# Nine seven-product steps in place of six, half of the other low parts by an accumulating DMA, and a new layout of the buffers

## The chip, the cores and the metric

The kernel runs on one core of one Trainium2 chip. The metric is the time of one execution on the device in microseconds (us). Three runs of the kernel before gave 1803.22, 1807.13 and 1808.31 us; the median is 1807.13 us.

## The reference

With DEPTH = 1 the reference computes one attention layer between two normalisations, in float32, for 256 positions and 4096 channels:

```python
h = x                                             # 256 x 4096
xn = rms_norm(h, norm_attn)
q, k, v, g = split(xn @ w_in, 4)                  # w_in 4096 x 16384
z = q_head @ k_head.T / sqrt(128)                 # 32 heads of 128
log_fail = where(causal, log_sigmoid(-z), 0)
a = where(causal, exp(log_sigmoid(z) + suffix_sums(log_fail)), 0)
h = h + ((a @ v_head) * silu(g)) @ w_out          # w_out 4096 x 4096
out = rms_norm(h, final_norm)
```

## The kernel before, in words

**Three matmuls for one product.** TensorE (PE) works on float32r operands, so each float32 operand is split into a high part (a cast) and a low part (what the cast lost). A product is `mm3`, L422 to L428: high times high, high of the input times low of the weights (`wl`), low of the input times high of the weights (`wh`), all 128x512 columns here. The high part of the weights is made by ScalarE (ACT) at L172, the low part by VectorE (DVE) through `minus`, L98.

**Units, steps, parts.** The work is a list of 21 units. Units 0 to 15 are the input projection, two for each group j of four heads: unit 2j gives q and k of the group, unit 2j+1 gate and v. Units 16 to 18 are the output projection, two blocks of 512 columns each; units 19 and 20 are one block each. I number the units from 0, so an odd unit below 16 is a gate-and-v unit. A unit has 16 steps s over the 4096 input channels; a step takes 256 channels and a quad of weights, 128 partitions x 4 x 512, loaded as `raw` (two DMAs of 512 KB on SP's queue, L150, three buffers).

A unit multiplies a 2 by 2 arrangement of blocks. Units 0 and 16 do it plainly, units 19 and 20 are single blocks, and the other 14 input units (2 to 15) and units 17 and 18 are mixed: in most steps eight products ("eight" steps, `EIGHT_PARTS`: two parts of 1024 columns), in the steps listed in `SEVEN` seven products of sums and differences of blocks ("seven" steps, `SEVEN_PARTS`: parts of 1024, 512, 1024 and 1024 columns). A seven step needs three additions of weight blocks by DVE, in place in `raw` (L160, L163, L164), ahead of its third part. Banks 1, 6 and 7 of PSUM hold sums that only seven steps add to; `combine_early` and `combine_late` (L346 to L363) put the banks together at a unit's end.

**What sets the order.** The loop at L687 walks through the parts. Before it issues the products of part n it calls `split` for as many later parts as the buffers allow: up to PAIRS = 4 parts of 1024 columns and SINGLES = 1 of 512, counted from part n. Work of the attention heads is hung on steps in a table `todo` (L569 to L664): transposes (`heads_T`), scores, sums (`weights_of`) and `heads_out` for each of the four heads of a group, the gate and the split of v. Each engine then runs its own instructions in a fixed order; the names `wl322`, `wh322` are the low and high part of part 322, `raw125` the quad 125. The heads' results go to DRAM (`spill`, L497), come back in units 15 and 16 as plain forms and as the seven forms (`build`, L213), and once more in unit 18.

## Time and profile before

| what | us |
|---|---|
| median of 3 runs | 1807.13 |
| the profiled execution | 1806.54 |
| its span, first to last instruction | 1804.6 |
| PE busy | 1778.2 |
| DVE busy | 1495.3 |
| ACT busy | 1089.5 |
| span of two mixed input units in the steady part | 177.1 |

The span lies 1.9 us under the execution's time; what happens in the trace is told from the span's start. Busy times of an engine count overlapping instructions once. Means of single instructions overlap their successors: the profile gives a matmul of 512 columns 390 ns, while matmuls start every 0.23 us.

### The profile page before, as it was taken

The numbers are of one execution on the slowest core, as the hardware profiler recorded it, in microseconds if no ns is written. First come the engines' busy times: TensorE is split into PE (matmuls) and PEld (weight loads), VectorE is DVE, ScalarE is ACT, GpSimd is POOL, SyncE is SP. The second block draws the span as 40 slices with busy tenths as digits, with TensorE's granted clock in tenths as the row PEclk, the third lists the DMA queues.
The fourth block names the chain that finished last, engine by engine and source line by source line (L and its number), as shares of the span: only waits on it lengthen the run. The fifth ranks groups of instructions, "written<-read, shape, count | busy, mean of one in ns | idle before, by whom it ended". The sixth has DMA issues, their size and how long they took to land. (4 is left out here: it accounts for less than half of the span.)

```text
span 1804.6 us, 22433 instructions
## 1 busy us (share of the span) xinstructions
PE 1778.2 (99%) x8107; PEld 1469.9 (81%) x8107; DVE 1495.3 (83%) x1810; ACT 1089.5 (60%) x1449; POOL 39.5 (2%) x80
## 2 busy tenths in 40 slices
PE   8999999999999999999999999999999999999997
PEld 6888788888888888888888888888887888788885
DVE  5678988888888888888888888888888977889854
ACT  5765665666566656665666565656565756655642
POOL 0000000000000000000000000000001011000000
PEclk9999999999999999999999999999999999999999
DMA  8856555555555545555555555555556666656664
GB/s 313 304 197 223 197 182 195 190 193 197 188 205 191 195 177 216 192 194 184 196 202 186 196 196 193 187 192 190 195 194 221 241 231 219 236 220 239 245 228 150
DMA packets 108814, 374.25 MB, mean 207 GB/s; under 512 B 12704, under 2 KB 12960, under 8 KB 108704
## 3 DMA queue, kind: packets, MB, share of 16 engines
q1 hardware_dynamic: 102960, 354.46, 54.8%
q0 software_dynamic: 5600, 18.35, 3.1%
q8 instruction: 63, 1.03, 0.2%
q14 instruction: 47, 0.39, 0.1%
q10 hardware_dynamic: 144, 0.02, 0.0%
HBM read 364.40 MB, written 8.39 MB: 207 GB/s over the span
## 5 line engine op out<-in xcount | busy, mean ns | idle before, releaser
L172 ACT CAST wh<-raw 128x1024 fp32r<-128x1024 f32 (+1 forms) x833 | 818.8, 1001 | 609.7 <-PE acc L428 274.8
L98 DVE TENSOR_TENSOR wl<-raw,wh 128x1024 fp32r<-128x1024 f32 (+1 forms) x833 | 950.6, 1159 | 245.0 <-ACT wh L172 236.5
L426 PE MATMUL acc<-wh,nh 128*128 128x512 f32 x1708 | 672.9, 394 | 2.2 <-ACT v_sb L383 1.9
L427 PE MATMUL acc<-wl,nh 128*128 128x512 f32 x1708 | 666.4, 390 | 2.7 <-DVE wl L98 2.3
L428 PE MATMUL acc<-wh,nl 128*128 128x512 f32 x1708 | 666.3, 390 | 0.0
L427 PEld LDWEIGHTS acc<-wl,nh 128*128 128x128 f32 x1708 | 321.1, 188 | 68.7 <-DVE wl L98 5.6
L428 PEld LDWEIGHTS acc<-wh,nl 128*128 128x128 f32 x1708 | 320.6, 188 | 68.0
L426 PEld LDWEIGHTS acc<-wh,nh 128*128 128x128 f32 x1708 | 320.9, 188 | 66.4 <-ACT v_sb L383 2.3
L426 PE MATMUL acc<-wh,ph 128*128 128x512 f32 x324 | 125.8, 390 | 2.1 <-ACT wh L172 1.5
L427 PE MATMUL acc<-wl,ph 128*128 128x512 f32 x324 | 126.5, 391 | 0.1
L428 PE MATMUL acc<-wh,pl 128*128 128x512 f32 x324 | 126.1, 389 | 0.0
L160 DVE TENSOR_TENSOR raw<-raw 128x1024 f32<-128x1024 f32 x96 | 117.4, 1223 | 2.3
L426 PE MATMUL acc<-wh,sh 128*128 128x512 f32 x256 | 101.3, 396 | 4.4 <-DVE sh L205 4.4
L427 PE MATMUL acc<-wl,sh 128*128 128x512 f32 x256 | 100.9, 394 | 0.7 <-DVE wl L98 0.6
L428 PE MATMUL acc<-wh,sl 128*128 128x512 f32 x256 | 100.4, 393 | 0.0
L426 PEld LDWEIGHTS acc<-wh,ph 128*128 128x128 f32 x324 | 60.7, 188 | 16.2 <-ACT wh L172 2.7
L427 PEld LDWEIGHTS acc<-wl,ph 128*128 128x128 f32 x324 | 60.8, 188 | 14.0 <-DVE wl L98 1.4
L428 PEld LDWEIGHTS acc<-wh,pl 128*128 128x128 f32 x324 | 60.8, 188 | 12.6
L164 DVE TENSOR_TENSOR raw<-raw 128x512 f32<-128x512 f32 x96 | 66.2, 690 | 2.4
L163 DVE TENSOR_TENSOR raw<-raw 128x512 f32<-128x512 f32 x96 | 66.1, 688 | 1.7
L426 PEld LDWEIGHTS acc<-wh,sh 128*128 128x128 f32 x256 | 48.7, 190 | 15.0 <-ACT wh L172 5.1
L427 PEld LDWEIGHTS acc<-wl,sh 128*128 128x128 f32 x256 | 48.8, 191 | 11.5 <-DVE wl L98 1.5
(167 smaller groups left out, 1374.1 us busy)
## 6 DMA issues: line engine op xcount, KB each, us to landing
raw<-in_w_in_dram SPq DMA_DIRECT2D x510, 512.0 KB, 4.2
raw<-in_w_out_dram SPq DMA_DIRECT2D x128, 512.0 KB, 4.2
xn<-in_xT_dram POOLq DMA_DIRECT2D x16, 256.0 KB, 3.0
xr<-in_x_dram SPq DMA_DIRECT2D x16, 256.0 KB, 5.0
spill<-gated POOLq DMA_DIRECT2D x16, 256.0 KB, 4.1
o<-spill POOLq DMA_DIRECT2D x16, 256.0 KB, 3.6
p<-spill POOLq DMA_DIRECT2D x16, 256.0 KB, 3.8
xres<-in_x_dram SPq DMA_DIRECT2D x16, 256.0 KB, 4.3
```

The lines of the kernel that those rows point to most:

```text
L98: nc.vector.tensor_tensor(out=out_, in0=full, in1=part.bitcast(F32), op=ALU.subtract)
L160: nc.vector.tensor_tensor(out=r[:, 0:3:2, :], in0=r[:, 0:4:3, :], in1=r[:, 2:3, :].broadcast_to([P, 2, CW]), op=ALU.add)
L163: nc.vector.tensor_tensor(out=r[:, 3, :], in0=r[:, 0, :], in1=r[:, 3, :], op=ALU.add)
L164: nc.vector.tensor_tensor(out=r[:, 1, :], in0=r[:, 3, :], in1=r[:, 1, :], op=ALU.add)
L172: nc.scalar.copy(wh[n][:, c, :], f)
L426: nc.tensor.matmul(out_, ah, bh, start=start, stop=False, **kw)
L427: nc.tensor.matmul(out_, ah, bl, start=False, stop=False, **kw)
L428: nc.tensor.matmul(out_, al, bh, start=False, stop=stop, **kw)
```

## The change

It does the following.

- `SEVEN` grows from six steps to nine (2, 3, 5, 6, 8, 9, 11, 12, 13) in units 2 to 15 and to eight in units 17 and 18 (`SEVEN_OUT`, without 12).
- In an eight step the low part of the second part of 1024 columns is no longer made by DVE. One quad ahead, ACT writes the negated high part into the buffer (`sum_up`, L165 of the changed kernel), and a DMA from GpSimd (POOL) adds the weights from DRAM to it with `accum_op` (L167). There are 114 such DMAs of 512 KB.
- The buffers of 1024 columns: four of high parts as before; three of low parts (`LOWS`) in place of four, and two more (`SUMMED`) that only the second part of a step other than a seven uses. The loop's condition counts them apart.
- Other tiles share buffers or get fewer: one buffer in place of two for `f`, four in place of five for `v`, the forms built in place of their source, the gate's transposes made head by head in `heads_out`, the scratch of the squares in PSUM.
- The heads' steps move: transposes at steps 5 and 10 of an odd unit in place of 2 and 8, and later steps in the next unit. Each pair of heads is now split once into high and low part (`heads_parts`) and stored in DRAM three times, so that the plain forms come back by DMA (`load_parts`) without a split; the forms of units 17 and 18 are built up to step 1 of unit 17.
- At the start x goes first: its first block on ACT's queue and ahead of all else, then weights and x by turns on SP's queue. The plain units copy bank 3 ahead of bank 7.

The diff, cut to what these points and the prediction speak of:

```diff
-SEVEN = (2, 4, 6, 9, 11, 13)
+SEVEN = (2, 3, 5, 6, 8, 9, 11, 12, 13)
+SEVEN_OUT = (2, 3, 5, 6, 8, 9, 11, 13)
 RAW_BUFS = 3
 PAIRS = 4
+LOWS = 3
+SUMMED = 2
 SINGLES = 1
...
+    summed = {p["quad"]: n for n, p in enumerate(parts) if p["summed"]}
+
+    def sum_up(q):
+
+        if q not in summed:
+            return
+        n = summed[q]
+        wl[n] = wp.tile([P, KT, CW], F32R, tag="wd", name=f"wl{n}", bufs=SUMMED)
+        nc.scalar.activation(wl[n], raw[q][:, parts[n]["place"], :], AF.Copy, scale=-1.0)
+        w, c, s = quads[q][1]
+        nc.gpsimd.dma_start(wl[n], w[c, s], accum_op=ALU.add)
+
     def split(n):
         p = parts[n]
         q = p["quad"]
         if p["i"] == 0 and (n == 0 or parts[n - 1]["quad"] != q):
             load(q + RAW_BUFS - 1)
+            sum_up(q + 1)
...
-        tag, bufs = ("w", PAIRS) if size == KT else ("one", SINGLES)
-        wh[n] = wp.tile([P, size, CW], F32R, tag=tag + "h", name=f"wh{n}", bufs=bufs)
-        wl[n] = wp.tile([P, size, CW], F32R, tag=tag + "l", name=f"wl{n}", bufs=bufs)
+        place, size = p["place"], p["size"]
+        (hi, hb), (lo, lb) = (("wh", PAIRS), ("wl", LOWS)) if size == KT else (("oneh", SINGLES), ("onel", SINGLES))
+        wh[n] = wp.tile([P, size, CW], F32R, tag=hi, name=f"wh{n}", bufs=hb)
+        if p["summed"]:
+            nc.scalar.copy(wh[n], r[:, place, :])
+            return
+        if p["apart"]:
+            lo, lb = "wd", SUMMED
+        wl[n] = wp.tile([P, size, CW], F32R, tag=lo, name=f"wl{n}", bufs=lb)
...
+        for k in range(KT):
+            nc.scalar.dma_start(xs[i][:, k, :], xT[i][:, k, :])
+            if k == 0:
+                nc.scalar.dma_start(gcol, gain_in)
...
-        for dst, r, col in ((one, r1, 1), (two, r2, 2)):
-            for t in range(NT):
...
+        for dst, r, col, t in ((one, r1, 1, 0), (one, r1, 1, 1), (two, r2, 2, 1), (two, r2, 2, 0)):
+            nc.scalar.activation(dst[t], bank[PLAIN[f"C{t + 1}{col}"]], AF.Copy, scale=r[:, t : t + 1])
...
-        for i, s in ((0, 2), (1, 8)):
+        for i, s in ((0, 5), (1, 10)):
             at(u + 1, s, heads_T, j, i)
             at(u + 1, s + 1, scores, j, i)
             at(u + 1, s + 3, weights_of, j, i)
...
-            inside = [len(range(*parts[m]["place"].indices(2 * KT))) for m in range(n, ready + 1)]
-            if inside.count(KT) > PAIRS or inside.count(1) > SINGLES:
+            inside = parts[n : ready + 1]
+            pairs = [m for m in inside if m["size"] == KT]
+            apart = sum(m["apart"] for m in pairs)
+            if len(pairs) > PAIRS or apart > SUMMED or len(pairs) - apart > LOWS or len(inside) - len(pairs) > SINGLES:
                 break
```

How this moves instructions is shown at one place on three engines: the end of step 12 and step 13 of unit 7, a gate-and-v unit in the steady part.

First DVE. Before, step 12 is an eight step (`wl318`, `wl319`) and step 13 a seven step on `raw125`; `a3_1` and `al3_1` belong to the group's second head:

```order
L98 TENSOR_TENSOR wl318_6026<-raw124_5927,wh318_6025 128x1024
L98 TENSOR_TENSOR wl319_6036<-raw124_5927,wh319_6035 128x1024
L98 TENSOR_TENSOR wl321_6056<-raw125_5953,wh321_6055 128x512
L98 TENSOR_TENSOR wl320_6052<-raw125_5953,wh320_6051 128x1024
L160 TENSOR_TENSOR raw125_5953<-raw125_5953 128x2x512
L466 TENSOR_TENSOR a3_1_6069<-a3_1_6069,bound_110 128x256
L163 TENSOR_TENSOR raw125_5953<-raw125_5953 128x512
L164 TENSOR_TENSOR raw125_5953<-raw125_5953 128x512
L98 TENSOR_TENSOR al3_1_6074<-a3_1_6069,ah3_1_6073 128x384
L98 TENSOR_TENSOR wl322_6081<-raw125_5953,wh322_6080 128x1024
L98 TENSOR_TENSOR wl323_6097<-raw125_5953,wh323_6096 128x1024
```

Of the change, where step 12 is a seven step too (ahead of these rows stand its first two low parts `wl352` and `wl353` with `qkl3_1` of the head between them, and its three additions):

```order
L101 TENSOR_TENSOR wl354_6252<-raw124_6143,wh354_6251 128x1024
L101 TENSOR_TENSOR wl355_6279<-raw124_6143,wh355_6278 128x1024
L448 SCALAR_TENSOR_TENSOR f3_1_6268<-z3_1_6261,f3_1_6268 128x384
L101 TENSOR_TENSOR wl356_6295<-raw125_6161,wh356_6294 128x1024
L450 TENSOR_TENSOR f3_1_6268<-f3_1_6268,bound_110 128x256
L101 TENSOR_TENSOR wl357_6302<-raw125_6161,wh357_6301 128x512
L178 TENSOR_TENSOR raw125_6161<-raw125_6161 128x2x512
L101 TENSOR_TENSOR fl3_1_6275<-f3_1_6268,fh3_1_6274 128x384
L181 TENSOR_TENSOR raw125_6161<-raw125_6161 128x512
L101 TENSOR_TENSOR wl358_6315<-raw125_6161,wh358_6314 128x1024
L182 TENSOR_TENSOR raw125_6161<-raw125_6161 128x512
L101 TENSOR_TENSOR wl359_6325<-raw125_6161,wh359_6324 128x1024
```

The additions of step 12 came in, the second half of the head's scores now stands between the parts of step 13, and the last addition L182 stands right before the last low part.

Next ACT, at the last high parts of step 13 (`wh322`, `wh323` before; `wh358`, `wh359` in the change). Before:

```order
L172 CAST wh322_6080<-raw125_5953 128x1024
L469 CAST ah3_1_6073<-a3_1_6069 128x384
L172 CAST wh323_6096<-raw125_5953 128x1024
L172 CAST wh324_6115<-raw126_6022 128x1024
L349 COPY v_sb3_0_6187<-acc7_1_5615 128x512
```

And in the change, where `wl363` is the negated high part of step 15:

```order
L194 CAST wh358_6314<-raw125_6161 128x1024
L364 COPY v_sb3_0_6420<-acc7_1_5806 128x512
L165 ACTIVATE wl363_6337<-raw127_6288 128x1024
L466 ACTIVATE a3_1_6375<-z3_1_6261 128x384
L365 ACTIVATE g_sb3_6419<-acc7_1_5806 128x512
L194 CAST wh359_6324<-raw125_6161 128x1024
```

Two copies of bank 1, a negation and a head's activation moved in front of the cast of the step's last part.

Last PE, at the end of step 13. `nh13` and `nl13` are the input's high and low part of step 13, `nh14` that of step 14. Before:

```order
L426 MATMUL acc7_4_5531<-wh323_6096,nh13_1679 128x512
L427 MATMUL acc7_4_5531<-wl323_6097,nh13_1679 128x512
L428 MATMUL acc7_4_5531<-wh323_6096,nl13_1680 128x512
L426 MATMUL acc7_6_5650<-wh323_6096,nh13_1679 128x512
L427 MATMUL acc7_6_5650<-wl323_6097,nh13_1679 128x512
```

In the change:

```order
L429 MATMUL acc7_4_5718<-wh359_6324,nh13_1672 128x512
L429 MATMUL acc7_6_5847<-wh359_6324,nh13_1672 128x512
L429 MATMUL acc7_2_5711<-wh360_6340,nh14_1738 128x512
L430 MATMUL acc7_4_5718<-wl359_6325,nh13_1672 128x512
L431 MATMUL acc7_4_5718<-wh359_6324,nl13_1673 128x512
L430 MATMUL acc7_6_5847<-wl359_6325,nh13_1672 128x512
```

Two matmuls that need only high parts, one of them of step 14, moved ahead of the first that needs the low part `wl359`.

More of the change, by code (lines that the diff above doesn't have):

```diff
@@ L131 @@
                     dict(u=u, s=s, i=i, last=i == len(which) - 1, place=place, prods=prods, quad=len(quads) - 1,
-                         seven=which is SEVEN_PARTS)
+                         seven=which is SEVEN_PARTS, summed=which is EIGHT_PARTS and i == 1,
+                         size=len(range(*place.indices(2 * KT))),
+                         apart=which is not SEVEN_PARTS and (s % 2 if kind == "single" else i) == 1)
                 )
@@ L262, in build_xn @@
             )
[L263 to L267 removed]
+        build(i, y, SEVEN, "n")
+    load_x(0)
+    load(0)
+    load_x(1)
+    load(1)
     load_x(2)
```

209 lines of the change are left out of this document (94 added, 115 removed).

## The prediction

> **What bounds the kernel now.** I read the page's first two lines first, then the table of waits for the whole core, then busy time by stretches.
>
> ```profile
> span 1804.6 us, 22433 instructions
> PE 1778.2 (99%) x8107; PEld 1469.9 (81%) x8107; DVE 1495.3 (83%) x1810; ACT 1089.5 (60%) x1449; POOL 39.5 (2%) x80
> ...
> ACT wh L172 <- PE acc L428: 274.8, 308, 2.5
> DVE wl L98 <- ACT wh L172: 236.5, 305, 3.0
> ...
> PE acc L426 <- DVE sh L205: 4.4, 1, 4.4
> ...
> PE acc L427 <- DVE wl L98: 2.9, 3, 1.4
> ...
> PE acc L426 <- ACT v_sb L383: 1.9, 1, 1.9
> ```
>
> PE is busy for 1778.2 of 1804.6 us. The long waits are those of the other engines: ACT waits 308 times until PE has freed a buffer of high parts, and DVE then waits for ACT. So both work as far ahead as their buffers let them, and PE sets the time. PE's own waits are a handful, 4.4 us of them at the start. Next, two stretches: two input units in the steady part, and one output unit.
>
> ```profile
> 446.50:623.60 177.10, 177.10 (x822) 147.58 (x821) 152.86 (x173) 109.43 (x140) 1.08 (x2) 1.00 0.54 194
> ...
> 1612.00:1695.00 83.00, 83.00 (x367) 68.44 (x366) 75.03 (x83) 49.03 (x62) 3.22 (x6) 1.00 0.67 237
> ```
>
> After the length come the busy times of PE, PEld, DVE, ACT and POOL, the granted clock and the DMA share. In 177.1 us PE never stops, and DVE is busy for 152.9. **PE's matmul count is the time here, and DVE has 24 us of room in two units.**
>
> **Term 1, matmuls taken away.** Three more sevens in each of 14 mixed input units and two more in each of two mixed output units: (14 x 3 + 2 x 2) x 3 = 138 matmuls of 512 columns fewer; the order of PE shows the same 138.
>
> ```profile
> 445.47 0.39 PE L427 MATMUL acc<-wl,nh 128*128 128x512 f32 x1
> ...
> 448.89 0.39 PE L427 MATMUL acc<-wl,nh 128*128 128x512 f32 x1
> ```
>
> These two starts lie 15 matmuls and 3.42 us apart, 0.228 us each (a mean of 390 ns overlaps the next one). 138 x 0.228 = **31.5 us less**, as long as PE stays fed. A seven step is 21 matmuls, 4.79 us; an eight step 24, 5.47 us.
>
> **Term 2, what DVE must now do, and when.** Durations overlap on DVE too, so I take the distance from start to start.
>
> ```profile
> 695.19 1.23 DVE L160 TENSOR_TENSOR raw<-raw 128x1024 f32<-128x1024 f32 x1
> 696.45 0.69 DVE L163 TENSOR_TENSOR raw<-raw 128x512 f32<-128x512 f32 x1
> ...
> 706.10 1.23 DVE L160 TENSOR_TENSOR raw<-raw 128x1024 f32<-128x1024 f32 x1
> 707.24 0.42 DVE L466 TENSOR_TENSOR a<-a,bound 128x256 f32<-128x256 f32 x1
> 707.58 0.69 DVE L163 TENSOR_TENSOR raw<-raw 128x512 f32<-128x512 f32 x1
> 708.30 0.69 DVE L164 TENSOR_TENSOR raw<-raw 128x512 f32<-128x512 f32 x1
> 708.91 0.55 DVE L98 TENSOR_TENSOR al<-a,ah 128x384 fp32r<-128x384 f32 x1
> 709.38 2.35 DVE L98 TENSOR_TENSOR wl<-raw,wh 128x1024 fp32r<-128x1024 f32 x2
> ...
> 715.70 1.22 DVE L98 TENSOR_TENSOR wl<-raw,wh 128x1024 fp32r<-128x1024 f32 x1 [0.79 <-ACT wh L172]
> 716.84 0.68 DVE L351 TENSOR_TENSOR v_sb<-acc,v_sb 128x512 f32<-128x512 f32 x1
> 717.44 1.22 DVE L98 TENSOR_TENSOR wl<-raw,wh 128x1024 fp32r<-128x1024 f32 x1
> ```
>
> A low part of 1024 columns takes 1.14 us (715.70 to 716.84), one of 512 takes 0.60, of 384 0.47, of 256 0.34. The three additions, each needing the one before, take 1.26 + 0.72 + 0.61 = 2.59 us; with other work between them 1.14 + 0.60 + 0.60. A seven step therefore costs DVE 3 x 1.14 + 0.60 + 2.59 = 6.6 us against PE's 4.79; an eight step costs it 2.28 before and 1.14 after the change (ACT and a DMA make the other low part), against 5.47. Over two input units DVE gains 2 x (3 x 2.59 + 3 x 0.60 - 4 x 1.14) = 10.0 us and two splits of heads (1.2): 152.9 + 11.2 = 164 of the 172.9 us that PE would need (177.1 - 18 x 0.228). As a sum it fits. **As an order it does not.** Sevens drain DVE's lead, and a lead is bounded by the buffers: three low parts and one single, that is one seven step. The eights 14, 15, 0, 1 leave DVE idle once those are full, and steps 2 to 13 hold nine sevens.
>
> I walk through the worst place, steps 11, 12, 13 of an odd unit, with the fullest lead: when PE starts step 11, DVE has all of 11. Its rows from there to the last low part of 13 (front part, first order block) are six of 1024 (6.84), two of 512 (1.20), additions 2.59 and 2.34, and the heads' 0.60 + 0.47 + 0.34 + 0.47 = 1.88: 14.85 us. It starts 1.30 us late, since the buffer of 12's first low part is that of 11's (four matmuls and 0.39), and before the last low part it waits for a cast that follows L182. The rows of ACT:
>
> ```profile
> 705.63 0.49 ACT L463 ACTIVATE a<-z 128x384 f32<-128x384 f32 x1 [0.82 <-PE z L460]
> ...
> 709.08 1.05 ACT L172 CAST wh<-raw 128x1024 fp32r<-128x1024 f32 x1 [0.26 <-DVE raw L164]
> ...
> 712.12 0.58 ACT L349 COPY v_sb<-acc 128x512 f32<-128x512 f32 x1
> ...
> 713.55 0.59 ACT L350 ACTIVATE g_sb<-acc 128x512 f32<-128x512 f32 x1
> ```
>
> So DVE ends at 1.30 + 14.85 + 1.05 = 17.2 us. PE wants that part after two steps (9.58), 15 matmuls (3.42), one more (0.23) and the heads' matmuls. For those:
>
> ```profile
> 404.99 0.28 PE L426 MATMUL o<-ah,vh 128*128 128x256 f32 x1
> ...
> 405.63 0.44 PE L426 MATMUL acc<-wh,nh 128*128 128x512 f32 x1
> ```
>
> Six such cost 0.64; a head's scores have the same shapes, its four sums about 0.6 (an estimate from this row). 9.58 + 3.42 + 0.23 + 0.64 + 0.6 = 14.5: DVE is 2.7 us late. In the changed order PE takes products with high parts ahead of their turn just there (third block), worth about three matmuls, 0.7: 2.0 us remain. The same sum in an even unit is 14.73 + 1.3 = 16.0 against 14.4, late by 1.6, and 0.9 after the products taken ahead. Mean of the two: 1.45.
>
> Two things come on top. ACT runs its queue in order, and the changed order has a cast of v, a negation, an activation of the head and a cast of g between the last two casts of high parts (second block): 1.05 + 0.58 + 1.05 + 0.49 + 0.59 = 3.76 us (the negation taken as a cast of its size) after L178, against 2.8 of DVE's work: 0.95 us in odd units, 0.5 in the mean. Behind that wait stand wh359, then wl359, then PE. And in the pairs 2-3, 5-6, 8-9 the same sum leaves 8.44 - (1.30 + 6.6) = 0.5 us, while up to 1.3 us of head work stands in them: from nothing to 0.9 late each, 1.2 per unit taken. So a unit is late by 1.45 + 0.5 + 1.2 = 3.15 us, **14 x 3.15 = 44 us more**. Bounds: 0.7 if the products taken ahead hide all but the triple, 5.9 if each wait of ACT for additions also stops DVE. The point of no gain is (31.5 + 5) / 14 = 2.6, the 5 from the next term. Output units have no such shortage: eight sevens there, and DVE has 8 of 83 us free.
>
> **Term 3, start and seams.**
>
> ```profile
> 8.97 0.35 DVE L205 TENSOR_SCALAR sh<-xs,gcol 128x256 fp32r<-128x256 f32 x1 [3.28 <-DMA xs<-in_xT_dram]
> ...
> 9.47 0.76 PE L426 MATMUL acc<-wh,sh 128*128 128x512 f32 x1 [4.35 <-DVE sh L205]
> ```
>
> The first product waits for x, queued on SP behind four weight loads; from ACT's queue it leaves about 2 us earlier: 3 us less with the loads that no longer stand before it, and 0 to 5 as bounds. The plain units free bank 3 one copy sooner (0.6 of the 1.9 us row above), and the forms of the output units come by DMA or are built later: 1.4. Together **5 us less**.
>
> **Term 4, the low part by DMA**, costed at nothing. It is covered by PE's work from the free buffer to its use: in a run of eights one step, half a step and a matmul, 5.47 + 2.74 + 0.23 = 8.4 us. To be hidden: a negation (1.05), the issue on POOL (0.54, the last row below) and the landing.
>
> ```profile
> raw<-in_w_in_dram SPq DMA_DIRECT2D x510, 512.0 KB, 4.2
> ...
> spill<-gated POOLq DMA_DIRECT2D x16, 256.0 KB, 4.1
> o<-spill POOLq DMA_DIRECT2D x16, 256.0 KB, 3.6
> ...
> L502 POOL DMA_DIRECT2D o<-spill x16: 536/536/543, 1297.2 to 1527.0; - x16
> ```
>
> No row shows an accumulating DMA. From below it is the plain load of its size, 4.2; from above that twice, for it reads its target too, 8.4. I take 5.5, nearer to the plain row: 7.1 of 8.4 us. At the upper end the part is 1.6 us late, in steps 0 and 1 of each unit. Behind such an accumulation on POOL's queue stand the next one and the spills; behind the negation on ACT stand the casts of the next step. The Trainium skill, page "DMA: Bandwidth & Descriptors", section "Anatomy of one DMA — SWDGE (gpsimd) path", gives 2.0 us plus the bytes at 436 GB/s for a DMA issued from GpSimd, 3.2 us by estimate at 512 KB; by that price the term stays nothing and rival 2 has no chance. It would make 2.6 of the 256 KB that take 3.6 and 4.1 in this trace, so the measured rows decide and rival 2 stays.
>
> **Sum**, against the profiled execution: 1804.6 - 31.5 + 44 - 5 = 1812 of span, and 1.9 around it (1806.5 - 1804.6): **1814 us**. The execution lies 0.6 under the median of 1807.1.
>
> **Rivals.**
> 1. Faster: the lead is enough. For it: DVE's sum fits with 9 us to spare, and PE's reordering may hide more than I count. Against: 2 us of the triple don't go away by it. With lateness between 0 and 2.2 us per unit: 1770 to 1801, about 1790.
> 2. Slower by far: the low part lands late. With 8.4 us landing, 2 x 1.6 x 14 = 45 us on top: 1859. It decides from a landing of 6.8 us on (8.4 - 1.6). For it: the DMA share is 0.54 already, and two units load 33.6 MB and get 7.3 MB more (14 low parts), read twice at worst.
> 3. Waits that halve the clock.
>
> ```profile
> 13.02 0.63 PE L426 MATMUL acc<-wh,sh 128*128 128x512 f32 x1
> 13.44 0.63 PE L427 MATMUL acc<-wl,sh 128*128 128x512 f32 x1
> ...
> 15.11 0.39 PE L427 MATMUL acc<-wl,sh 128*128 128x512 f32 x1
> 15.34 0.40 PE L428 MATMUL acc<-wh,sl 128*128 128x512 f32 x1
> ...
> 9.40:14.00 4.60, 4.53 (x11) 3.60 (x12) 4.60 (x7) 3.24 (x6) 0.00 (x0) 0.50 1.04 409
> ...
> 194.00:200.00 6.00, 4.12 (x18) 3.08 (x18) 4.07 (x6) 6.00 (x11) 0.00 (x0) 1.00 0.49 175
> ```
>
> After the 4.35 us wait at the start, matmuls come every 0.42 us at a clock of 0.50, from 9.47 to about 15 us; 5.4 us at that pace instead of 0.228 lose 2.5. The 1.9 us wait for v_sb, in the last row, leaves the clock at 1.00. If the lateness of an odd unit fell together into one wait of 4 us, it would cost 7 x 2.5 = 18 us: 1832. The Trainium skill, page "TensorE: Matmul & The Clock Gate", section "Part 1: The HAM clock gate", says that an idle window of about 3.4 us brings half the clock; the trace agrees at the start, and by that rule a wait of this length in each odd unit would be enough.
>
> That the change does not do what it says I leave out: its 138 matmuls and 114 accumulating DMAs stand in the order.
>
> **Numbers.** Forecast 0.47 (its own range 1803 to 1832), rival 1 0.30, rival 2 0.15, rival 3 0.08. The range leaves out the faster end of rival 1 (0.1) and the far end of rival 2 (0.08): 1780 to 1858, which are also lateness of 0.7 and about 6 us per unit. About 0.3% (5.4 us) is what a measurement can tell from no change: faster 0.30; the part of the forecast under 1812.5 is same, 0.13; slower 0.34 + 0.15 + 0.08 = 0.57.
>
> **What would show it.** Two input units last 173 us if rival 1 holds fully, 177 at no gain, 179 by my sum. PE should wait for wl and wh in steps 12 and 13, up to 2.7 us at a time, nothing of that in steps 14 to 1; DVE should idle there and be busy for 164 us of two units. Waits of PE for DMA wl mean rival 2; a clock under 0.99 in the steady part, rival 3. I am wrong if DVE's steps are shorter than 6.6 us, or if it enters step 11 with more than one step of lead.

## The result, and the profile after

| | before | after |
|---|---|---|
| median of 4 runs each, us | 1805.99 | 1935.51 |
| ratio, 95% interval | | 1.0719, 1.0698 to 1.0739 |
| span of the profiled execution, us | 1804.6 | 1933.4 |
| PE busy, matmuls | 1778.2, 8107 | 1820.3, 7969 |
| DVE busy, us | 1495.3 | 1564.3 |
| ACT busy, us | 1089.5 | 1253.9 |

The kernel has its 138 matmuls fewer and takes 129.5 us more. The page of after, its first lines, its line of the granted clock, and parts 3, 4 and 6 (in part 6 the last column is the median from issue to landing):

```profile
span 1933.4 us, 23059 instructions
PE 1820.3 (94%) x7969; PEld 1448.0 (75%) x7969; DVE 1564.3 (81%) x1940; ACT 1253.9 (65%) x1670; POOL 169.6 (9%) x251
...
PEclk9999999999999999999999999999999899899998
...
q1 hardware_dynamic: 102672, 354.20, 50.8%
q0 software_dynamic: 31696, 93.08, 23.3%
...
PE 32%; issue 28%; DVE 15%; DMA 14%; ACT 8%; POOL 1%; SPq 0%; ACTq 0%; DVEq 0%; POOLq 0%
...
raw<-in_w_in_dram SPq DMA_DIRECT2D x510, 512.0 KB, 5.3
...
wl<-in_w_in_dram POOLq DMA_DIRECT2D x98, 512.0 KB, 6.8
```

PE was busy for 99% of the span and is now for 94%. Without the 138 matmuls its busy time should have fallen by 31.5 us, and it rose by 42.1: a matmul's row (0.39 us) is longer than the distance to the next (0.228), so short waits and a slower clock hide in busy time. The idle part of the span grew from 26.4 to 113.1 us. The last chain of work runs through DVE, DMA and ACT for more than a third of its length. A weight load lands in 5.3 us where it took 4.2; the accumulating DMA takes 6.8. Next, two input units and one output unit (columns as in the prediction):

```profile
661.10:851.40 190.30, 178.89 (x792) 141.22 (x790) 160.96 (x188) 128.06 (x166) 14.57 (x19) 0.99 0.74 224
...
1728.00:1823.00 95.00, 86.73 (x366) 67.31 (x364) 73.02 (x80) 56.11 (x69) 15.35 (x24) 1.00 0.93 280
```

Two input units take 190.3 us where PE's own work is 173.0 (177.1 - 18 x 0.228), and the output unit 95 for 83. The DMA share went from 0.54 to 0.74 and from 0.67 to 0.93. What the engines waited for (total us, times, longest), PE's weight loads, PE and ACT:

```profile
PEld acc L430 <- DVE wl L101: 65.5, 92, 4.2
PEld acc L429 <- ACT wh L194: 50.0, 64, 3.3
PEld acc L430 <- DMA wl<-in_w_in_dram: 20.0, 17, 2.5
PEld o L429 <- ACT gated L497: 17.9, 25, 2.1
```

```profile
PE acc L430 <- DVE wl L101: 28.1, 44, 3.8
PE acc L429 <- ACT wh L194: 26.1, 32, 2.9
...
PE z L429 <- DVE qkl L101: 5.7, 2, 4.9
...
PE acc L429 <- DVE sh L231: 1.4, 1, 1.4
```

```profile
ACT wh L194 <- DVE raw L178: 225.0, 122, 2.7
ACT wh L194 <- PE acc L431: 125.9, 120, 2.0
ACT wl L165 <- DMA raw<-in_w_in_dram: 71.4, 44, 6.1
...
ACT wh L194 <- DMA raw<-in_w_in_dram: 24.8, 14, 4.8
...
ACT wl L165 <- DMA raw<-in_w_out_dram: 15.7, 9, 5.9
```

ACT's wait for PE, the sign of a full lead, fell from 274.8 to 125.9 us. The first line, the wait for a seven's additions, is 204.7 us in before. New is the third line: **ACT stands at the negation (L165) for 71.4 us because the next quad has not landed.** How that reaches PE can be read in one place. ACT, DVE and PE around 855 us, start, duration, and in brackets the idle time before and what ended it:

```profile
851.08 1.06 ACT L194 CAST wh<-raw 128x1024 fp32r<-128x1024 f32 x1
854.29 1.06 ACT L165 ACTIVATE wl<-raw 128x1024 fp32r<-128x1024 f32 x1 [2.15 <-DMA raw<-in_w_in_dram]
855.25 1.03 ACT L194 CAST wh<-raw 128x1024 fp32r<-128x1024 f32 x1
```

```profile
856.31 1.23 DVE L101 TENSOR_TENSOR wl<-raw,wh 128x1024 fp32r<-128x1024 f32 x1 [2.75 <-ACT wh L194]
```

```profile
856.33 0.51 PE L429 MATMUL acc<-wh,nh 128*128 128x512 f32 x1 [1.04 <-ACT wh L194]
857.59 0.50 PE L430 MATMUL acc<-wl,nh 128*128 128x512 f32 x1 [0.75 <-DVE wl L101]
...
859.36 0.63 PE L430 MATMUL acc<-wl,nh 128*128 128x512 f32 x1
859.78 0.63 PE L431 MATMUL acc<-wh,nl 128*128 128x512 f32 x1
```

```profile
858.90:861.90 3.00, 3.00 (x8) 2.32 (x7) 2.08 (x3) 2.09 (x5) 0.00 (x0) 0.50 0.98 250
```

ACT is free at 852.14, but the negation stands first in its program and waits 2.15 us for a quad of a later step. The cast behind it comes late by that and by the negation itself, DVE waits 2.75 us for the cast, PE 1.04 for the cast and 0.75 for the low part. Then the matmuls come every 0.42 us for a while instead of every 0.228: the granted clock is 0.50 in these three us (last row, columns as before).

For the comparison of kernels I cut every profiled execution at the same row of DVE, the first `q_sb<-acc` of `combine_late` after units 2 and 14. In after:

```profile
292.16 0.69 DVE L373 SCALAR_TENSOR_TENSOR q_sb<-acc,q_sb 128x512 f32<-128x512 f32 x1 [1.03 <-PE acc L431]
...
1435.89 0.69 DVE L373 SCALAR_TENSOR_TENSOR q_sb<-acc,q_sb 128x512 f32<-128x512 f32 x1 [1.06 <-PE acc L431]
```

Between them lie twelve mixed input units (3 to 14), 1143.7 us, 95.3 each; in before the rows stand at 281.55 and 1344.03, 88.5 each. "Start" is what lies ahead: units 0 to 2, of which unit 1 is as plain as unit 0. "Rest" runs from there to the same kind of row of `h` after unit 18; the tail behind that is 101 to 106 us in all. Where I speak of one unit or step alone, I cut at PE's matmuls, whose number in each is fixed. An experiment has two runs (six_dve three, before7 and before7in ten). They ran on several chips, where before's median lay between 1804.4 and 1806.4 us, so differences of 2 us between rows of the table say nothing. In the kernel seven_dve, which the table leaves out, the profiled one of two runs had a clock of 0.75 throughout (2205.09 us), so only its other run is used below.

| kernel | time, us | ratio to before, 95% interval | start | twelve units | each | rest |
|---|---|---|---|---|---|---|
| before | 1805.99 | | 281.6 | 1062.5 | 88.5 | 358.3 |
| six_dve | 1818.36 | 1.0072 (1.0049 to 1.0095) | 287.6 | 1066.6 | 88.9 | 359.0 |
| eight_dve | 1831.80 | 1.0152 (1.0123 to 1.0182) | 287.5 | 1073.3 | 89.4 | 365.2 |
| nine_dve | 1862.63 | 1.0310 (1.0280 to 1.0340) | 290.7 | 1100.5 | 91.7 | 367.9 |
| nine_rooms5 | 1866.15 | 1.0341 (1.0311 to 1.0371) | 289.3 | 1105.9 | 92.2 | 367.4 |
| free_low | 1841.77 | 1.0206 (1.0174 to 1.0238) | 283.3 | 1088.2 | 90.7 | 364.5 |
| plain_dma | 1844.37 | 1.0220 (1.0191 to 1.0250) | 287.2 | 1088.2 | 90.7 | 365.0 |
| acc_no_neg | 1873.82 | 1.0385 (1.0350 to 1.0420) | 297.2 | 1088.6 | 90.7 | 383.8 |
| no_dma | 1876.65 | 1.0388 (1.0358 to 1.0418) | 289.0 | 1104.3 | 92.0 | 377.3 |
| chain_plain | 1881.43 | 1.0415 (1.0395 to 1.0436) | 290.2 | 1104.6 | 92.1 | 382.5 |
| neg_const | 1892.48 | 1.0486 (1.0453 to 1.0519) | 287.0 | 1113.8 | 92.8 | 383.7 |
| neg_aside | 1931.20 | 1.0701 (1.0679 to 1.0722) | 296.5 | 1124.5 | 93.7 | 403.7 |
| half_first | 1931.39 | 1.0692 (1.0671 to 1.0713) | 293.0 | 1140.5 | 95.0 | 393.5 |
| after | 1935.51 | 1.0719 (1.0698 to 1.0739) | 292.2 | 1143.7 | 95.3 | 395.2 |
| six_acc | 1867.68 | 1.0338 (1.0308 to 1.0368) | 293.9 | 1092.7 | 91.1 | 378.2 |
| pool_neg | 2013.82 | 1.1159 (1.1101 to 1.1218) | 292.8 | 1200.8 | 100.1 | 420.2 |
| neg_wh | 2437.35 | 1.3508 (1.3469 to 1.3547) | 312.8 | 1521.0 | 126.8 | 499.0 |
| before7 | 1804.36 | 0.9988 (0.9978 to 0.9997) | 279.4 | 1055.2 | 87.9 | 364.7 |
| before7in | 1805.31 | 1.0004 (0.9993 to 1.0014) | 282.6 | 1055.3 | 87.9 | 360.0 |

What each kernel changes is told in the next section. With six sevens PE's matmuls set the time, as in before; with nine they would make 88.5 - 9 x 0.228 = 86.5 us a unit.

### The profile page after: what moved, and what is told of

The parts are those of the page before. It is cut to its first block, busy times and chain, and to the rows that moved or that the text cites. A ratio compares the mean times of both kernels' runs of the same rounds, so it can differ in the third digit from the quotient of the medians.

```text
span 1933.4 us, 23059 instructions
## 1 busy us (share of the span) xinstructions
PE 1820.3 (94%) x7969; PEld 1448.0 (75%) x7969; DVE 1564.3 (81%) x1940; ACT 1253.9 (65%) x1670; POOL 169.6 (9%) x251
## 3 DMA queue, kind: packets, MB, share of 16 engines
q0 software_dynamic: 31696, 93.08, 23.3%
## 4 chain that ended last, share of the span: by engine, by line
PE 32%; issue 28%; DVE 15%; DMA 14%; ACT 8%; POOL 1%; SPq 0%; ACTq 0%; DVEq 0%; POOLq 0%
PE acc L430 11%; PE acc L431 10%; PE acc L429 10%; DMA raw<-in_w_in_dram 9%; DVE wl L101 8%; ACT wh L194 6%; DVE raw L178 3%; DMA wl<-in_w_in_dram 3%; DMA raw<-in_w_out_dram 2%; DVE raw L182 1%; DVE raw L181 1%; DMA xn<-in_xT_dram 1%; ACT wh L187 1%; ACT wl L165 1%; POOL wl L167 1%
## 5 line engine op out<-in xcount | busy, mean ns | idle before, releaser
L101 DVE TENSOR_TENSOR wl<-raw,wh 128x1024 fp32r<-128x1024 f32 (+1 forms) x811 | 902.4, 1127 | 232.6 <-ACT wh L194 215.0
L194 ACT CAST wh<-raw 128x1024 fp32r<-128x1024 f32 (+1 forms) x811 | 771.9, 971 | 437.2 <-DVE raw L178 225.0
L429 PE MATMUL acc<-wh,nh 128*128 128x512 f32 x1666 | 654.5, 402 | 18.4 <-ACT wh L194 18.4
L431 PE MATMUL acc<-wh,nl 128*128 128x512 f32 x1666 | 657.0, 394 | 0.0
L429 PEld LDWEIGHTS acc<-wh,nh 128*128 128x128 f32 x1666 | 313.6, 190 | 96.9 <-ACT wh L194 35.9
L165 ACT ACTIVATE wl<-raw 128x1024 fp32r<-128x1024 f32 x114 | 120.8, 1060 | 100.1 <-DMA raw<-in_w_in_dram 71.4
L167 POOL DMA_DIRECT2D wl<-in_w_in_dram x98 | 85.0, 867 | 1116.3 <-ACT wl L165 933.9
L178 DVE TENSOR_TENSOR raw<-raw 128x1024 f32<-128x1024 f32 x142 | 173.5, 1222 | 1.8
L187 ACT CAST wh<-raw 128x1024 fp32r<-128x1024 f32 x114 | 118.8, 1042 | 1.1 <-PE acc L431 1.0
L181 DVE TENSOR_TENSOR raw<-raw 128x512 f32<-128x512 f32 x142 | 98.0, 690 | 3.6
L182 DVE TENSOR_TENSOR raw<-raw 128x512 f32<-128x512 f32 x142 | 98.0, 690 | 3.4
```

Source lines behind the costliest of these rows:

```text
L101: nc.vector.tensor_tensor(out=out_, in0=full, in1=part.bitcast(F32), op=ALU.subtract)
L165: nc.scalar.activation(wl[n], raw[q][:, parts[n]["place"], :], AF.Copy, scale=-1.0)
L167: nc.gpsimd.dma_start(wl[n], w[c, s], accum_op=ALU.add)
L178: nc.vector.tensor_tensor(out=r[:, 0:3:2, :], in0=r[:, 0:4:3, :], in1=r[:, 2:3, :].broadcast_to([P, 2, CW]), op=ALU.add)
L181: nc.vector.tensor_tensor(out=r[:, 3, :], in0=r[:, 0, :], in1=r[:, 3, :], op=ALU.add)
L182: nc.vector.tensor_tensor(out=r[:, 1, :], in0=r[:, 3, :], in1=r[:, 1, :], op=ALU.add)
```

## The experiments

My theory was the prediction's: sevens beside each other make DVE and ACT late. The main rival was the accumulating DMA; a third was the new layout. The first three kernels make, with after, the four corners (nine or six sevens, with or without accumulations); the fourth drops the DMA alone.

**Six sevens, accumulations kept.**

```diff
-SEVEN = (2, 3, 5, 6, 8, 9, 11, 12, 13)
-SEVEN_OUT = (2, 3, 5, 6, 8, 9, 11, 13)
+SEVEN = (2, 4, 6, 9, 11, 13)
+SEVEN_OUT = (2, 4, 6, 9, 11, 13)
```

> The changed kernel with the six steps of before in seven products (2, 4, 6, 9, 11, 13), in input and output units alike; ten low parts a mixed unit now come by the accumulating DMA instead of seven. Theory 1 (the sevens' chain of additions, casts and low parts on DVE and ACT is late, as I predicted it but larger): the lateness goes with the triple and the pairs, DVE has more room than in the kernel before, and the time is that of before or a little under, 1795 to 1815 us. Theory 2 (the accumulating DMA: its negation blocks ACT, its part lands late, its traffic delays the raw parts): there are 10/7 as many of them, the time stays above 1900 and may pass 1935. Theory 3 (each a share): between, 1840 to 1890.

1867.68 us: theory 3, each a share. DVE was busy for 71% only, so accumulations cost without any shortage of DVE. There are 160 of them here, 114 in after.

**Nine sevens, no accumulation; and six sevens, no accumulation** (the latter with the diff above as well).

```diff
-    summed=which is EIGHT_PARTS and i == 1,
+    summed=False,
```

> The changed kernel with its nine and eight sevens, but every low part made by DVE: no negation on ACT, no accumulating DMA. DVE gets 14 low parts of about 1.27 us more in two input units, 164 + 18 = 182 us. Theory 1 (DVE late): worse than after, 2000 to 2050 us, since DVE keeps the 26 us of waiting that it has now in a pair of 190. Theory 2 (the accumulating DMA is what is late): the waits go, two units take DVE's 182 us and some, which makes 1880 to 1935; the output units, where DVE has room, go from 95 to 108 us back to 83 to 87 in any case of theory 2 and not in theory 1.

> The changed kernel with the six sevens of before and every low part by DVE: what is left of the change is the new layout of rooms, the start, the heads' work and LOWS 3 for 4. Theories 1 and 2: 1795 to 1815 us. A third theory (three rooms for low parts, the gate's transposes and copies beside the products, one room for f): the loss stays, over 1850.

1862.63 and 1818.36 us. The second lies 3 us above its 1795 to 1815: the layout costs 12 us. The first is faster than either theory allowed: DVE did not keep its waits, it worked through them.

```profile
PE 1794.5 (96%) x7969; PEld 1442.0 (77%) x7969; DVE 1674.5 (90%) x2054; ACT 1150.3 (62%) x1556; POOL 69.4 (4%) x137
```

So taking low parts off DVE made the kernel 73 us slower, and DVE's load is not what makes after so late.

**No accumulating DMA, negation kept.**

```diff
         nc.scalar.activation(wl[n], raw[q][:, parts[n]["place"], :], AF.Copy, scale=-1.0)
-        w, c, s = quads[q][1]
-        nc.gpsimd.dma_start(wl[n], w[c, s], accum_op=ALU.add)
```

> The changed kernel without the accumulating DMAs alone: ACT writes the negated high part as before, which the products then use as the low part (so the low parts of these products are left out, their time is not). ACT's negation still waits for the raw part. Theory 1: DVE and ACT do what they did, 1915 to 1940 us. Theory 2 by landing or traffic: 1790 to 1830 us. Theory 2 by ACT's blocked order alone (the negation waits for a raw part one step ahead): raw parts come sooner with 75 MB less traffic, but most of the loss stays, 1870 to 1920.

1876.65 us, as forecast for ACT's blocked order alone: 59 of the 129.5 us are the DMA's. In the twelve units PE, DVE and ACT run the same instructions in the same order in both kernels, so nothing but the DMA differs there. The rest of this kernel's loss was then taken apart.

**Low parts that cost nothing; plain DMAs with no negation.**

```diff
-        nc.scalar.activation(wl[n], raw[q][:, parts[n]["place"], :], AF.Copy, scale=-1.0)
-        nc.gpsimd.dma_start(wl[n], w[c, s], accum_op=ALU.add)
...
             nc.scalar.copy(wh[n], r[:, place, :])
+            wl[n] = wh[n]
```

```diff
-        nc.scalar.activation(wl[n], raw[q][:, parts[n]["place"], :], AF.Copy, scale=-1.0)
-        nc.gpsimd.dma_start(wl[n], w[c, s], accum_op=ALU.add)
+        nc.gpsimd.dma_start(wl[n], w[c, s].bitcast(F32R))
```

> After's kernel with nine and eight sevens in which the low parts that the change takes off DVE cost nothing at all: no negation, no DMA, the products take the high part a second time (the low parts of these products are left out). DVE has its 164 us of two units, ACT 14 us less than after. My theory of the prediction (DVE late in the triple and the pairs, 3.15 us a unit): 1786 + 44 = about 1815 to 1835 us. A theory in which only the accumulation was late: 1785 to 1800. A theory in which casts wait for additions whatever DVE's load (the chain of a seven is too long for three rooms of low parts): 1850 to 1880, like the kernel with DVE's low parts (1862.63).

> After's kernel with the negation on ACT left out and the accumulating DMA made a plain one into the same room: as many bytes and as many issues on POOL, but nothing that waits for a raw part (the low part of these products is then a copy of the whole weight, so their low parts are left out of the result, not of the time). If the 75 MB of traffic itself is what costs (raw parts landing in 5.3 us for 4.2): above 1900 us. If the chain costs (raw part, negation on ACT, accumulation, product): 1840 to 1876 us, no more than without the DMA (1876.65), since the negation is gone as well.

1841.77 and 1844.37 us. In both kernels the low parts of these products are left out of the result. 60 MB more by plain DMAs (93.08 against 33.30 MB on POOL's queue; the expectations' 75 MB is the difference to before) cost nothing that can be told from none, although raw parts land in 5.5 us there and in 4.5 without: traffic alone is not it. The first lies between my theory's 1835 and the chain theory's 1850. Sevens are late by 90.7 - 86.5 = 4.2 us a unit even with DVE relieved at no price; nine_dve, with 7 x 1.14 = 8 us more for DVE in each unit, is 1.0 us later still.

**Negation on POOL; five rooms for low parts in one rotation.**

```diff
-        nc.scalar.activation(wl[n], raw[q][:, parts[n]["place"], :], AF.Copy, scale=-1.0)
+        nc.gpsimd.tensor_scalar(wl[n], raw[q][:, parts[n]["place"], :], -1.0, None, op0=ALU.mult)
```

```diff
-LOWS = 3
+LOWS = 5
...
-        if p["apart"]:
+        if False:
             lo, lb = "wd", SUMMED
```

The second has `summed=False` as well.

> After's kernel with the negation made by POOL in place of ACT; the accumulating DMA stands behind it on the same engine as before. If ACT's program blocked behind a negation that waits for a raw part carries the loss of the DMAs (ACT waited 100 us so): the time falls from 1935 to 1870 to 1895 us. If the landing of the accumulation carries it: 1915 to 1945 us, or later still, by as much as POOL is slower at a negation than ACT's 1.06 us and shares DVE's way to memory.

> Nine and eight sevens, all low parts by DVE, and the five rooms for low parts in one rotation instead of three and two (the same room in memory). If three rooms for a seven's low parts make the lateness: 1862.63 falls to 1820 to 1845 us. If DVE's own 183 us of work in two units do: 1855 to 1866 us.

2013.82 us: a negation on POOL takes 3.16 us in the mean, and PE waits 72.5 us for the accumulation behind it in the input units, against 13.3 in after.

```profile
L165 POOL TENSOR_SCALAR wl<-raw 128x1024 fp32r<-128x1024 f32 x114 | 360.7, 3164 | 977.9 <-DMA raw<-in_w_in_dram 589.4 <-PE acc L430 190.3 <-PE acc L431 92.0
```

It shows that the lead is small, not what ACT's blocking costs. One more room for a seven's low parts (1866.15 against 1862.63) is no help; more is not tested, for `PAIRS` = 4 bounds the lead in both.

**Accumulation with no negation ahead of it; negation from the high part, behind its cast.**

```diff
-        wl[n] = wp.tile([P, KT, CW], F32R, tag="wd", name=f"wl{n}", bufs=SUMMED)
-        nc.scalar.activation(wl[n], raw[q][:, parts[n]["place"], :], AF.Copy, scale=-1.0)
+        wl[n] = rooms_wd[order_wd[q] % SUMMED]
         w, c, s = quads[q][1]
         nc.gpsimd.dma_start(wl[n], w[c, s], accum_op=ALU.add)
```

```diff
-            sum_up(q + 1)
...
             nc.scalar.copy(wh[n], r[:, place, :])
+            sum_up(q)
...
-        nc.scalar.activation(wl[n], raw[q][:, parts[n]["place"], :], AF.Copy, scale=-1.0)
+        nc.scalar.activation(wl[n], wh[n].bitcast(F32), AF.Copy, scale=-1.0)
```

> After's kernel without the negation: the DMA still accumulates, as many bytes and issues, but onto whatever two fixed rooms hold, so it waits for no raw part and for nothing of ACT, only for the products that read the room before (the low parts of these products are left out of the result). If an accumulating transfer is dear by itself (its queue took 23.3% of the engines for 93 MB where plain ones took 16.1%): 1880 to 1935 us. If the chain raw part, negation on ACT, accumulation, product is what costs: 1840 to 1855 us, as with plain DMAs (1844.37).

> After's kernel with the negation taken from the high part, right behind its cast, instead of from the raw part a step ahead: correct, with the same work on every engine, ACT never stands at a negation that waits for a raw part, but the accumulation starts later. If ACT's blocked program carries the accumulation's loss (94 us over the kernel in which it is free): 1860 to 1895 us. If the landing before the product carries it: 1935 to 2000 us, with PE's waits for the accumulating DMA above the 33 us of after.

1873.82 us, between the two expectations. The twelve units are those of free_low to 0.5 us; the loss lies in the start (+14) and the rest (+19). Two of its input units, and unit 18:

```profile
663.10:844.40 181.30, 177.15 (x802) 142.58 (x801) 162.71 (x191) 118.56 (x155) 15.49 (x20) 1.00 0.76 235
...
1688.10:1772.60 84.50, 83.15 (x362) 67.14 (x361) 72.38 (x80) 48.78 (x58) 13.89 (x22) 1.00 0.97 297
```

DMA share 0.76, clock 1.00, no time lost in the input units: free_low takes 181.3 us for two as well. **Accumulating DMAs that nobody's program waits for are free in the twelve input units.** A high DMA share alone costs nothing in unit 18 either: 84.5 us at 0.97, against 83.9 in free_low and 94.4 in after at 0.93. What is lost lies in units 0 and 1 (+12), 16 (+7) and 17 (+11). Units 0, 1 and 16 are plain and have no such DMA; but this edit leaves the low parts of plain units three rooms in place of five, and DVE's two clearings of the rooms stand at the start. So what accumulations cost outside the twelve units is not shown by this kernel.

The second kernel took 2437.35 us:

```profile
PEld acc L430 <- DMA wl<-in_w_in_dram: 376.9, 76, 8.2
PEld acc L430 <- DMA wl<-in_w_out_dram: 62.0, 14, 7.1
```

That is far past both expectations. Begun at the cast, the accumulation lands up to 8 us after PE wants it. After needs its negation a step early, and pays for that on ACT.

**Eight sevens without step 12; seven sevens, none beside another** (both `summed=False`).

```diff
-SEVEN = (2, 3, 5, 6, 8, 9, 11, 12, 13)
+SEVEN = (2, 3, 5, 6, 8, 9, 11, 13)
```

```diff
-SEVEN = (2, 3, 5, 6, 8, 9, 11, 12, 13)
-SEVEN_OUT = (2, 3, 5, 6, 8, 9, 11, 13)
+SEVEN = (2, 4, 6, 8, 10, 12, 14)
+SEVEN_OUT = (2, 4, 6, 8, 10, 12, 14)
```

> Nine sevens become eight in the input units (step 12 goes back to eight products, so that there is no triple), all low parts by DVE. PE gets 14 x 0.684 = 9.6 us more of matmuls than in the kernel with nine (1862.63). If the triple at steps 11 to 13 makes most of the sevens' lateness (4.8 us a unit in the kernel with free low parts, 3.2 of it in the last 8 us): 14 x 3.2 = 45 us go, 1862.6 + 9.6 - 45 = 1825 to 1832 us. If the lateness is spread over all pairs or is DVE's whole load: 1850 to 1870 us.

> Seven sevens in steps of their own (2, 4, 6, 8, 10, 12, 14), in input and output units, all low parts by DVE, on after's layout. One seven a unit more than the kernel with six (1818.36): 18 x 0.684 = 12 us less of matmuls. If only neighbouring sevens are late: 1803 to 1810 us. If each seven past six costs more than its 0.684 us whatever its place: 1818 to 1835 us.

1831.80 us, as forecast for the triple: with step 12 an eight again the kernel is 30.8 us faster although PE gets 9.6 us more to do. The triple costs 40 / 14 = 2.9 us a unit of nine_dve's 91.7 - 86.5 = 5.2. seven_dve took 1811.75 us, between its expectations: 6.6 us under six_dve, half of the 12 expected, on a chip where before is 1.8 us faster.

**Start the chain sooner; end it sooner.** The half of a quad that is negated is loaded first; and a plain DMA overwrites what ACT wrote.

```diff
-        for k, (w, c, s) in enumerate(quads[q]):
+        for k, (w, c, s) in sorted(enumerate(quads[q]), reverse=q in summed):
```

```diff
-        nc.gpsimd.dma_start(wl[n], w[c, s], accum_op=ALU.add)
+        nc.gpsimd.dma_start(wl[n], w[c, s].bitcast(F32R))
```

> After's kernel, in which the half of a raw part that is to be negated is loaded first of the two, so that negation, accumulation and landing can all begin about one transfer sooner (a little over 1 us of SP's two issues and of the landing); ACT's program has some negations one cast earlier. If the accumulation's lead decides (raw part, negation, accumulation, product): at least a quarter of the 59 us between after and the kernel without the DMA goes, 1895 to 1920 us. If its traffic on the engines' queues decides: 1930 to 1940 us.

> After's kernel with the negation on ACT kept and the DMA behind it a plain one, that overwrites what ACT wrote (the low parts of these products are left out of the result): the same chain, 4.1 us of landing instead of 6.8 and 16% instead of 23% of the DMA engines' time. If the chain's length decides by its last part: 2.7 us less on it, 1885 to 1910 us. If the chain as such costs whatever its end (ACT at a negation that waits for a raw part delayed by more traffic): 1920 to 1940 us. If only accumulating transfers cost: 1876 us, as without any DMA.

1931.39 us: no help, as forecast for traffic and against the lead theory. ACT's program changed with it in many places, and its waits for quads at negations even grew:

```profile
ACT wl L165 <- DMA raw<-in_w_in_dram: 82.2, 34, 6.8
```

So the sum of these waits is no price by itself: six_acc has 114.7 us of them and loses less.

1881.43 us, 5 above no_dma: with a plain DMA in the same chain the twelve units are those of no_dma (92.1 against 92.0). The order of PE, DVE and ACT there is the same in after, no_dma and chain_plain, so **the step from 92.1 to 95.3 us a unit is made by the accumulation alone.** The waits of ACT for quads at negations are 42.0 us in chain_plain, and 33.3 with no DMA at all:

```profile
ACT wl L165 <- DMA raw<-in_w_in_dram: 42.0, 34, 3.4
```

```profile
ACT wl L165 <- DMA raw<-in_w_in_dram: 33.3, 27, 3.1
```

**ACT's wait without the chain; the chain without the wait.** To acc_no_neg comes a copy by ACT of the same half quad onto itself at the negation's place; and in after the negation reads a constant column.

```diff
         wl[n] = rooms_wd[order_wd[q] % SUMMED]
+        half = raw[q][:, parts[n]["place"], :]
+        nc.scalar.activation(half, half, AF.Copy)
```

```diff
-        nc.scalar.activation(wl[n], raw[q][:, parts[n]["place"], :], AF.Copy, scale=-1.0)
+        nc.scalar.activation(
+            wl[n].rearrange("p a b -> p (a b)"), gcol[:, 0:1].broadcast_to([P, KT * CW]), AF.Copy, scale=-1.0
+        )
```

> The kernel with accumulations onto fixed rooms and no negation (1873.82), with ACT's work and wait put back beside them: ACT copies the same half of the same raw part onto itself at the place where it negated it in after, so it stands there until the raw part has landed, but no accumulation and no product hangs on it (the low parts of these products are left out of the result). If after's loss is ACT's blocked program, made worse by raw parts that land later beside accumulating transfers: 1925 to 1945 us, as after. If it is the chain negation, accumulation, product: 1873.8 plus the 35 us that the negation cost without any DMA, 1900 to 1912 us.

> After's kernel, in which ACT's negation reads a constant column in place of the raw part: the same 114 ACT instructions of about 1.06 us, the accumulation behind each and the product behind that, but no wait for a raw part (the low parts of these products are left out of the result). If the wait for the raw part makes the loss, on ACT or in the chain: 1870 to 1885 us, near the accumulations without a negation (1873.82). If ACT's 121 us of work do, or the chain from ACT to the product: 1900 to 1935 us.

1931.20 us: as long as after, with no accumulation behind ACT. In the total this flatters the theory, for the start and the rest are worse than after's, and this kernel has acc_no_neg's three rooms for plain units too. In the twelve units neg_aside has 36 of the 55.5 us that after has over free_low. They don't lie at the same place: of its 3.0 us a unit 2.0 fall in step 12, where after loses 0.5; and the copies stand elsewhere in ACT's program than after's negations, some of them earlier. So it shows that such a wait can cost this much, not that it is after's share. ACT's wait:

```profile
ACT raw L170 <- DMA raw<-in_w_in_dram: 58.2, 43, 4.3
```

1892.48 us, between the two expectations: with the chain and ACT's work but no wait for a quad, 43 us go, 30 of them in the twelve units. ACT's program has another order here too, and ACT waits 50.0 us for PE at these negations, so this kernel does not isolate the wait.

**A version that might beat both:** the kernel before with seven sevens apart everywhere, and with seven in the input units and six in the output units. Both have three rooms for low parts.

```diff
-SEVEN = (2, 4, 6, 9, 11, 13)
+SEVEN = (2, 4, 6, 8, 10, 12, 14)
...
-        wl[n] = wp.tile([P, size, CW], F32R, tag=tag + "l", name=f"wl{n}", bufs=bufs)
+        wl[n] = wp.tile([P, size, CW], F32R, tag=tag + "l", name=f"wl{n}", bufs=min(bufs, 3))
```

```diff
+SEVEN_OUT = (2, 4, 6, 8, 10, 12)
...
-                    which = SEVEN_PARTS if s in SEVEN else EIGHT_PARTS
+                    which = SEVEN_PARTS if s in (SEVEN if w is w_in else SEVEN_OUT) else EIGHT_PARTS
```

> The kernel before with seven sevens (2, 4, 6, 8, 10, 12, 14) for six, none beside another, and three rooms for low parts instead of four to make room for the seventh form. 18 x 0.684 = 12 us less of matmuls. If only neighbouring sevens are late, and three rooms are enough: 1793 to 1799 us, faster than both kernels. If the lost room or DVE's 3 us more a unit cost: 1800 to 1812 us.

> The kernel before with seven sevens apart (2, 4, 6, 8, 10, 12, 14) in the input units alone and six (2, 4, 6, 8, 10, 12) in the output units, three rooms for low parts. The kernel with seven everywhere was 7.2 us shorter in the twelve steady input units and 2.2 at the start than before, and 6.4 us longer behind them. If the output units' seventh seven made those 6.4: 1794 to 1798 us, faster than both kernels. If the third room for low parts did: 1803 to 1806 us.

1804.36 and 1805.31 us: neither is a gain that counts. The twelve units are 7.3 and 7.2 us shorter, of 8.2 in matmuls; the first loses 6.4 in the rest, the second 1.0 at the start, 1.7 in the rest and 3.7 in the tail. Why it is given back there stays open.

## Why the prediction was wrong

The direction was right, and the size was not: 129.5 us more where I had forecast 8, beyond the range. Within after's layout the loss adds up by medians: layout and order 12.1 (six_dve), matmuls -31.5, sevens 54.9 (free_low against six_dve, matmuls added back), negation on ACT 34.9 (no_dma), accumulating DMA 58.9 (after); the sum is 129.3, as it must be, for each kernel is set against the one before it. The forecast had -5, -31.5, 44 and nothing for the last two. The shares hold for this order of removal: in place of low parts by DVE, negation and DMA cost 72.9 us with nine sevens (after against nine_dve, 114 of them) and 49.3 with six (six_acc against six_dve, 160).

- **Term 4, "costed at nothing", is the step that failed**: 94 us. Its row-bounds held: landing 6.8 us, inside 4.2 to 8.4, though I took 5.5; the issue on POOL 0.87, not 0.54 (the row was a plain DMA). The profile counts landing from the issue's start, so my sum had the issue twice; with the measured rows it is 1.06 + 6.8 = 7.9 of 8.4 us by the median (the slowest landed in 9.6). But I asked only whether the part reaches PE in time, which is rival 2. I wrote that "behind the negation on ACT stand the casts of the next step" and gave it no price. The negation reads a quad that is a step away, and ACT runs in order. In the twelve units, per unit: the sevens and the layout bring 86.5 to 90.7; the negation alone 1.3; the accumulating DMA behind it 3.3, to 95.3. Both the longer wait at the negation (neg_aside has 1.7 over no_dma) and the accumulation's own lateness (the weight loads' 20.0 us of waits for it, rival 2's sign) are in these 3.3; how they share them is not shown. Of the 95 us between the spans of free_low and after, 55.5 lie in the twelve units, 8.9 in the start and 30.7 in the rest, there mostly in units 15, 17 and 18.
- **Why accumulating ones and not plain ones.** Plain transfers of the same bytes delay raw parts about as much (landing in 5.5 us in plain_dma, 4.9 in chain_plain, 5.3 in after) and cost the twelve units nothing; in unit 18 the plain chain does cost, 91.3 us against no_dma's 85.7. With accumulating ones ACT's waits at negations rise from 42.0 to 71.4 us. Which property does it, the 23% of the engines' time against 16%, or the longer landing, isn't separated.
- **Term 2, 3.15 us a unit, was right in mechanism and small in size**: 90.7 - 88.9 + 2.05 = 3.9 measured with the layout taken out, within 0.7 to 5.9. The triple was forecast as most of it, and it is 2.9 of 5.2 in nine_dve; it was not taken out of free_low. (The rows counted for steps 12 and 13 are those of the second order block, not of the first.) DVE's 164 us of two units came as forecast: 163.0 to 163.4 from one `q_sb` row to the next. "Output units have no such shortage" was right for DVE and wrong for the unit: it went from 83 to 95 us, with DVE less busy. Cut at PE's matmuls, unit 18 takes 83.2 us in before, 83.9 in free_low, 85.7 in no_dma, 93.1 in neg_aside and 94.4 in after: there too the loss comes with the negation beside transfers.
- **Term 1** held: 138 matmuls, and PE's pace unchanged where it is fed.
- **Term 3, -5, was wrong in sign**: six_dve is 6.0 us late at the start. Unit 0 is 5.2 us shorter there, and the first product comes 3 us sooner (PE's wait for `sh` is 1.4 us in after instead of 4.4); but unit 1 is 8.8 us longer and unit 2 2.4. In after PE waits 5.7 us for a head's low part `qkl` in unit 1, as in six_dve. Two kernels with before's start gave 279.4 and 282.6, so a us or two of this is scatter.
- **Rival 3 joined in.** By PE's rows 121 matmuls of 512 columns into the accumulators last 0.6 us or more in after, 66 in no_dma, 15 in free_low, 12 in before; at 0.42 - 0.228 = 0.2 us each that is some 24 us of after's time, against 2 in before. It needed no wait of 4 us, and it follows the waits: it is part of the shares above.
- **What would show it**: I expected PE to wait in steps 12 and 13 and not in 14 to 1. Of the 4.6 us a unit that after has over free_low, 1.5 fall in steps 12 and 13, 2.2 in 14, 0 and 1, 0.7 in step 2. Whether DVE enters step 11 with more than one step of lead stays open.

## What to carry to other kernels

On an engine that runs its program in order, work taken over for a later step is paid not only by its duration but by what it waits for: ask which of its inputs may be late, and who stands behind it. A transfer is not free because its bytes fit; look at who needs the transfers that it delays, and how early. And when an engine looks short (DVE here), check by an experiment that relieves it for nothing before paying to relieve it: here nine sevens were slower than six (1841.77 against 1818.36 us) even with half the low parts of the eight steps for free.

## What the runs showed of the hardware

An accumulating DMA of 512 KB from POOL landed in 6.8 us in the input units (with no negation ahead of it in 5.4, and in 8.1 in the output units), a plain one from the same queue in 4.1; POOL spent 0.87 us on its issue, 0.53 on a plain one's. The queue's share of the 16 engines was 23.3% against 16.1% for 93.08 MB. The Trainium skill, page "DMA: Bandwidth & Descriptors", section "Anatomy of one DMA — SWDGE (gpsimd) path", has a formula that makes 3.2 us of 512 KB, an estimate; neither kind agrees, and the measured rows decide.

The clock fell after short waits: in after, waits of 0.68, 0.53 and 2.16 us between 752.4 and 758.3 us were followed by a stretch with a clock of 0.60, in which matmuls came every 0.42 us, and then it stood at 1.00 again.

```profile
753.00:758.00 5.00, 2.54 (x9) 1.45 (x9) 2.47 (x4) 3.82 (x6) 0.86 (x1) 1.00 0.20 80
759.00:763.00 4.00, 3.79 (x10) 2.86 (x10) 3.11 (x4) 3.57 (x5) 0.00 (x0) 0.60 0.98 269
764.00:768.00 4.00, 4.00 (x19) 3.28 (x18) 2.07 (x3) 2.41 (x4) 0.00 (x0) 1.00 1.03 420
```

PE was busy for 2.54 of the 5 us in the first row. The Trainium skill, page "TensorE: Matmul & The Clock Gate", section "Part 1: The HAM clock gate", speaks of an idle window of about 3.4 us that halves the clock; no single wait here is that long, so the trace agrees only if several short waits can make up a window, which no run tested.
